# Two rates of a background stream of weight sums: 2.4 in place of 3.2 a tile before the first norm, 0.75 in place of 0.72 an item in the MLP

## The chip, the core and the metric

The kernel runs on one core of a Trainium2 chip. The metric is the time of one execution in microseconds (us), taken on the device; the time given for a kernel is the median of several runs. Before the change it is 1033.77 us (median of 3 runs, 1033.19 to 1034.73).

## What is computed

One layer of a decoder trunk on 512 tokens of width 1024, all in float32. The parts that matter here come after the three attention mixers:

```python
merged = (g[:, :, 0] * (o_da @ w_branch_da) + g[:, :, 1] * (o_sb @ w_branch_sb)
          + g[:, :, 2] * (o_dl @ w_branch_dil))
m = merged @ w_out
x = layer_norm(DEEPNORM_ALPHA * x + m, ln1_g, ln1_b)           # the first norm
hid = jax.nn.relu(x @ w_up)                                    # 1024 -> 4096
c = jnp.square(hid) @ w_down                                   # 4096 -> 1024
ple = jax.nn.sigmoid(x @ w_ple_gate) * (p @ w_ple)
x = layer_norm(DEEPNORM_ALPHA * x + c + ple, ln2_g, ln2_b)
```

## The kernel before, in words

**Products.** A float32 product is made of three TensorE (PE) products: each operand is cast to a rounded high part (ScalarE, ACT) and the rest is taken as its low part (VectorE, DVE); high times high, high times low and low times high are added up in PSUM. Large products are also split into quadrants and done with seven products of half size instead of eight (Strassen's scheme). For that the kernel needs sums and differences of weight quadrants, beside the weights themselves.

**Weight stream.** SyncE (SP) loads weights in chunks of 128x1024 (512 KB) into six buffers `raw`, in the order of use (line 213). For each chunk ACT makes `wh` (line 262) and DVE makes `wl` (line 264); of both there are five buffers. A buffer `raw` comes free when its `wl` is done, and the next load of SP waits for that.

**Sum steps.** The sums of weights are not made by the compute engines but by the DMA queue of GpSimd (POOL): `sum_steps()` (from line 1212) yields one DMA a step. A step copies 512 KB of a weight, or of an earlier sum, into a buffer in DRAM (line 1249), or adds 512 KB to it (line 1247). Buffers are `usum` for w_up, `dsum` for w_down, `gsum`, `qsum`, `msum`, `bsum` and `vsum` for others; eight steps make the four sums of one block of w_up or w_down, and 208 steps are issued in all. SP later loads such sums as chunks. A step that reads or adds to a buffer has to wait until the DMA before it on this buffer has landed. The wait is held by POOL, which takes its instructions strictly in their written order: whatever stands behind the step waits too. Besides, each step waits for the fourth last `wl` that was recorded before it, which spreads the steps over time.

**Order of the work.** The program is a list of items; an item is one PE product of a tile with what prepares it and what takes it out of PSUM. The main loop (from line 2177) walks through the items, and keeps a `credit`: before each item it adds `size * rate` (items 5 up to five behind the start of the output projection) or a constant (items from seven behind the start of the `w_ple` product to the end), and for each whole unit it issues one step. Between the two stretches, around the first norm, none is issued. The output projection starts at item 162, the `w_ple` product at item 174, the MLP's first item is near 200, and there are some 320 items. So the rate that the output projection's tiles carry counts only for its first five items, which are tile 0, two small transposes, tile 1 and one small transpose.

**The first norm.** For each of the four tiles of 128 tokens, `layer_norm_act` (from line 992) is: DVE makes the mean (`lnm`, line 997), ACT the squares (line 999), DVE the variance (`lr`, lines 1001 and 1002), POOL the power -1/2 of `lr` (line 1003, one 128x1 operation), DVE the result `xn` (line 1013, two instructions). `ln1_gen` then lets PE transpose the tile (line 1078, eight small products with `ident`), ACT cast it (`x1hT`, line 1084), DVE make its low part (`x1lT`, line 1085), and ACT copy it for the quadrants (`x1r`, line 1091). The gate product of the PLE branch (lines 1169 to 1171) comes next on PE; between the tiles' transposes stand the `w_ple` products (lines 1109 to 1111).

**POOL's other DMAs there.** `ln_g`, `ln_b` (line 988) and `pTr` (line 1780) are loads of constants; line 176 adds a quadrant of the gate's weights onto a `raw` buffer once its first form has been cast.

The two lines that the change touches, with what stands around them:

```python
item(cs if tt == 3 else [], mm, ev, need=cs, bank=at_bank)
items[-1]["rate"] = 3.2
...
if 5 <= n < wout_at + 5:
    credit += it["size"] * it.get("rate", 1.0)
elif n > ple_at + 6:
    credit += 0.72
while credit >= 1:
    credit -= 1
    next(sum_steps_, None)
```

Of the kernel before, what the change touches and what calls it, by code (L numbers as in the profile page):

```python
# [55 lines left out]
def trunk(tc, a, out):  # L56
    nc = tc.nc
    es = ExitStack()
    with es:
# [17 lines left out]
        def small(name, n):  # L77
            return one.tile([P, n], F32, name=nm(name), tag=f"sm{n}", bufs=12 if n < 8 else 8)
# [89 lines left out]
        def chunk(src, w):  # L168
            return chunk_of(load(src, w))
# [104 lines left out]
        def pump(limit, most=2):  # L274
            n = 0
            while n < most and st["split"] < len(chunks) and (chunks[st["split"]].get("aside")
                                                              or st["ring"] < limit + RING):
                fill()
                issue_split()
                n += 1  # L280
            fill()


        items = []

        def item(cs, mm, ev, need=None, bank=None, size=1.0):
            items.append({"c": cs, "mm": mm, "ev": ev, "need": need, "bank": bank, "size": size})
# [385 lines left out]
        def bring_back(i):  # L673
            for k in range(4 * i, 4 * i + 4):
                oT[k] = slot("oT")
                nc.sync.dma_start(oT[k], kept_oT.pop(k))
# [268 lines left out]
        def turn_item(h, th, kp):  # L945
            def mm(ps):
                for k in range(2):
                    for t in range(2):
                        o, c = k * 256 + t * P, (2 * kp + k) * P
                        nc.tensor.transpose(ps[:, o:o + P], merged[2 * th + t, h][:, c:c + P], ident)  # L950

            def ev(ps):
                hi, lo = slot("mh", F32R), slot("ml", F32R)
                nc.scalar.copy(hi, ps)
                nc.vector.tensor_sub(lo, ps, hi.bitcast(F32))
                merged_T[h, th, kp] = (hi, lo)
            item([], mm, ev, size=0.08)
# [70 lines left out]
        def wout_items():  # L1028
            for half in range(2):
                cs = [chunk(a["wo"][half, c].rearrange("p k n -> p (k n)"), 1024) for c in range(4)]  # L1030
                for tt in range(4):
                    ks = (4, 5, 6, 7, 0, 1, 2, 3) if tt == 2 and not half else range(8)

                    def mm(ps, tt=tt, cs=cs, ks=ks):
                        for k in ks:
                            c = cs[k // 2]
                            s = slice((k % 2) * 512, (k % 2) * 512 + 512)
                            h, lo = merged_T[k // 4, tt // 2, k % 4 // 2]
                            q = slice(k % 2 * 256 + tt % 2 * P, k % 2 * 256 + tt % 2 * P + P)
                            nc.tensor.matmul(ps, h[:, q], c["h"][:, s], start=k == ks[0], stop=False)  # L1040
                            nc.tensor.matmul(ps, h[:, q], c["l"][:, s], start=False, stop=False)
                            nc.tensor.matmul(ps, lo[:, q], c["h"][:, s], start=False, stop=k == ks[-1])

                    def ev(ps, tt=tt, half=half):
                        y = xn.pop((tt, half))
                        if not half:
                            x1sum[tt] = small("lsm", 2)
                        i = nc.vector.scalar_tensor_tensor(y, y, ALPHA, ps, op0=OP.mult, op1=OP.add,
                                                           accum_out=x1sum[tt][:, half:half + 1])
                        st["added"] = getattr(i, "ins", i)  # L1050
                        x1[tt, half] = y
                        if half:
                            pending.append(ln1_gen(tt))
                    item(cs if tt == 3 else [], mm, ev, need=cs, bank=at_bank)
                    items[-1]["rate"] = 3.2
                    for t in {0: [(1, 1, 0), (1, 1, 1)], 1: [(0, 1, 0), (0, 1, 1)]}.get(tt, ()) if not half else ():
                        turn_item(*t)

# [731 lines left out]
        def split_oT(i):  # L1790
            for k in range(4 * i, 4 * i + 4):
                oTs[k] = split(oT.pop(k), "oT")
# [348 lines left out]
        def step():  # L2141
            done = len(nc.cur_bb.bb.instructions)
            step_heads()
            for i in nc.cur_bb.bb.instructions[done:]:
                if i.engine in (mybir.EngineType.Activation, mybir.EngineType.DVE):
                    heads_last[i.engine] = i
            if tied[0]:
                tie[:] = list(heads_last.values())
# [24 lines left out]
        credit = 0.0  # L2173
# [3 lines left out]
        for n, it in enumerate(items):  # L2177
            if n == forms_at:
                pending.append(mixer_forms())
            if n == gated_at - 1:  # L2180
                while active or waiting:
                    step()
            for i in range(3):
                if i and n == branch_at[i] - (0, 9, 14)[i]:
                    bring_back(i)
                if n == branch_at[i] - (8, 2, 8)[i]:
                    while any(k not in ready for k in range(4 * i, 4 * i + 4)):
                        step()
                    if i == 1:
                        split_oT(i)  # L2190
                    else:
                        pending.append(branch_forms(i))
            need = it["need"] or it["c"]
            while any("h" not in c for c in need):
                before = st["split"]
                pump(freed, 1)
                assert st["split"] > before, n
            if prev is not None:
                prev[0]["ev"](prev[1])
                todo, lead = prev[0].get("then", ((), 0))  # L2200
                preps.extend(todo)
                for _ in range(lead):
                    left_step(*preps.popleft())

            pump(freed, {1: 3, 3: 0, 4: 0, ple_at: 0, ple_at + 1: 0}.get(n, 1 if n < 10 else 2))
            if n == 8:
                tie.clear()
            tied[0] = pair_at[1] + 12 <= n < gated_at
            if n == gated_at:
                tie.clear()  # L2210
            if n == 4:
                with tc.issue_after(st["load"]):
                    load_consts()
            if n == 10:
                with tc.issue_after(st["low"]):
                    make_lam()
            if n == 9:
                load_onehot()
            if n == 13:
                pending.append(tables())  # L2220

            if 5 <= n < wout_at + 5:
                credit += it["size"] * it.get("rate", 1.0)
            elif n > ple_at + 6:
                credit += 0.72
            while credit >= 1:
                credit -= 1
                next(sum_steps_, None)
            if n == 22:
                turn_tables()  # L2230
            if n == DA_TABS:
                da_tables()
            if n == DA_TABS + 6:
                turn_da()
            if n == wout_at + 1:
                load_pT()
            if n == ple_at - 3:
                with tc.issue_after(st["added"]), tc.issue_after(st["cast"]):
                    split_pT()
            if n == wout_at - 8:  # L2240
                load_xn(0)
            if n == wout_at - 4:
                load_xn(1)
            if n == wout_at - 1:
                ln_consts("ln1_g", "ln1_b")
            if n == ln2_at[0]:

                ln_consts("ln2_g", "ln2_b")
            for j in (n, n + 1):
                if j < len(items) and items[j].get("pre"):  # L2250
                    items[j].pop("pre")()
            if n > 1:
                step()
            ps = it["bank"]() if it["bank"] else mm_bank()
            for _ in it["mm"](ps) or ():
                if HALF:
                    step()
            freed += sum(not c.get("aside") for c in it["c"])

            pump(freed, 0 if n < 10 or ple_at - 1 <= n <= ple_at + 1 or n in sums_first else 2)  # L2260
            prev = (it, ps)
            if n + 1 < len(items) and n >= wout_at and pending:
                pass
# [113 lines left out]
```

## Time and profile before

| what | value |
|---|---|
| median of 3 runs | 1033.77 us (1033.19 to 1034.73) |
| the profiled execution's own time | 1031.9 us |
| its span, first to last instruction | 1030.2 us |
| granted TensorE clock, mean over the span | 0.997 |
| PE busy | 1016.4 us (99%) |
| DVE busy | 796.5 us (77%) |
| ACT busy | 614.7 us (60%) |
| POOL busy | 208.5 us (20%) |
| moved by DMA | 275.99 MB, 268 GB/s in the mean |
| POOL's DMA queue (q0) | 135.08 MB, 52.1% of 16 engines' span |
| SP's DMA queue (q1) | 138.99 MB, 36.8% |

The profiled execution is one of its own, 1.87 us below the median of the runs; 1.7 us of its time lie outside the span. Busy time of PE is modelled from the starts of pipelined products, so that products of 0.39 us each follow one another every 0.23 us. In a row of the timeline stand the start, the duration, engine, line, operation and tiles; "idle before" tells how long the engine had nothing to run, and what ended that. Buffer numbers are left out of tile names there.

### The profile page before, as it was taken

The page shows a single profiled execution, that of the slowest core. Times are in us where ns is not written, and L with a number is a line of the kernel's source. Part 1 is how long each engine was busy: PE and PEld are TensorE (multiplying, and loading weights), DVE is VectorE, ACT ScalarE, POOL GpSimd, SP SyncE. Part 2 cuts the span into 40 slices and gives each one's busy share as a digit, 9 for nine tenths or more (in the row PEclk, how much of TensorE's full clock was granted, in tenths as well). Part 3 has the DMA queues.
Part 4 walks back from the last instruction along what each step waited for, and adds up shares of the span by engine and source line. Part 5 has one row for each costly group of instructions (what it writes and reads, how often), then busy time and mean ns, then how long its engine had stood idle before and what let it go on. Part 6 is the DMA issues. An engine that isn't in the chain of part 4 may idle for free.

```text
span 1030.2 us, 15635 instructions
## 1 busy us (share of the span) xinstructions
PE 1016.4 (99%) x5626; PEld 880.8 (86%) x5626; DVE 796.5 (77%) x1411; ACT 614.7 (60%) x1055; POOL 208.5 (20%) x311
## 2 busy tenths in 40 slices
PE   9999999999999999999999999899999999999997
PEld 7888887788998898888888888789999899899886
DVE  6888697788657777787788876697768777777975
ACT  7566566775544656556655733776666556556651
POOL 0322320121412224111221140221121212111101
PEclk9999999999999999999999999999999999999999
DMA  8999993888899999989999994789999999999922
GB/s 311 282 308 287 254 269 103 208 209 266 275 322 276 274 279 273 286 222 299 284 270 299 305 306 162 171 236 333 322 322 345 301 347 306 328 313 292 310 79 82
DMA packets 79885, 275.99 MB, mean 268 GB/s; under 512 B 9816, under 2 KB 10600, under 8 KB 79808
## 3 DMA queue, kind: packets, MB, share of 16 engines
q0 software_dynamic: 37712, 135.08, 52.1%
q1 hardware_dynamic: 41520, 138.99, 36.8%
q8 instruction: 44, 0.72, 0.3%
q10 hardware_dynamic: 576, 0.92, 0.2%
q14 instruction: 33, 0.27, 0.1%
HBM read 267.59 MB, written 116.42 MB: 373 GB/s over the span
## 4 chain that ended last, share of the span: by engine, by line
PE 88%; DVE 3%; DMA 3%; issue 2%; ACT 2%; POOL 1%; DVEq 0%; POOLq 0%; ACTq 0%
PE mm L87 9%; PE mm L88 9%; PE mm L89 9%; PE at L1430 4%; PE at L1431 4%; PE at L1432 4%; PE at L750 2%; PE at L752 2%; PE at L751 2%; PE at L89 2%; PE at L88 2%; PE at L87 2%; PE mm L750 2%; PE mm L752 2%; PE mm L751 2%
## 5 line engine op out<-in xcount | busy, mean ns | idle before, releaser
L264 DVE TENSOR_TENSOR wl<-raw,wh 128x1024 fp32r<-128x1024 f32 (+1 forms) x274 | 330.3, 1214 | 105.0 <-ACT wh L262 103.7
L262 ACT CAST wh<-raw 128x1024 fp32r<-128x1024 f32 (+1 forms) x274 | 284.4, 1043 | 206.0 <-PE mm L88 104.3
L87 PE MATMUL mm<-xhT,wh 128*128 128x512 f32 (+1 forms) x254 | 95.5, 376 | 1.1 <-DVE dl_k L346 1.1
L89 PE MATMUL mm<-xhT,wl 128*128 128x512 f32 (+1 forms) x254 | 94.3, 371 | 0.0
L88 PE MATMUL mm<-xlT,wh 128*128 128x512 f32 (+1 forms) x254 | 94.1, 370 | 0.0
L1430 PE MATMUL at<-wh,hh 128*128 128x512 f32 x188 | 73.7, 392 | 0.0
L1431 PE MATMUL at<-wl,hh 128*128 128x512 f32 x188 | 73.7, 392 | 0.0
L1432 PE MATMUL at<-wh,hl 128*128 128x512 f32 x188 | 73.1, 389 | 0.0
L87 PE MATMUL mm<-x1hT,wh 128*128 128x256 f32 x256 | 72.8, 284 | 0.3 <-ACT up L1358 0.3
L89 PE MATMUL mm<-x1hT,wl 128*128 128x256 f32 x256 | 72.4, 283 | 0.0
L88 PE MATMUL mm<-x1lT,wh 128*128 128x256 f32 x256 | 72.4, 283 | 0.0
L87 PEld LDWEIGHTS mm<-xhT,wh 128*128 128x128 f32 x254 | 47.9, 189 | 8.9 <-issue 1.2
L89 PEld LDWEIGHTS mm<-xhT,wl 128*128 128x128 f32 x254 | 47.8, 188 | 8.2
L88 PEld LDWEIGHTS mm<-xlT,wh 128*128 128x128 f32 x254 | 47.9, 189 | 7.5
L1247 POOL DMA_DIRECT2D usum<-in_wu_dram x32 | 27.5, 861 | 120.8 <-DVE wl L264 43.9
L87 PEld LDWEIGHTS mm<-x1hT,wh 128*128 128x128 f32 x256 | 48.9, 191 | 2.3 <-ACT up L1358 0.5
L88 PEld LDWEIGHTS mm<-x1lT,wh 128*128 128x128 f32 x256 | 48.9, 191 | 1.5
L89 PEld LDWEIGHTS mm<-x1hT,wl 128*128 128x128 f32 x256 | 48.9, 191 | 0.0
L1247 POOL DMA_DIRECT2D dsum<-in_wd_dram x28 | 23.1, 824 | 120.4 <-DMA dsum<-dsum 32.4
L1432 PEld LDWEIGHTS at<-wh,hl 128*128 128x128 f32 x188 | 35.3, 188 | 7.6
L1430 PEld LDWEIGHTS at<-wh,hh 128*128 128x128 f32 x188 | 35.5, 189 | 6.2
L1431 PEld LDWEIGHTS at<-wl,hh 128*128 128x128 f32 x188 | 35.5, 189 | 5.7
(676 smaller groups left out, 2859.8 us busy)
## 6 DMA issues: line engine op xcount, KB each, us to landing
usum<-in_wu_dram POOLq DMA_DIRECT2D x48, 512.0 KB, 10.1
dsum<-in_wd_dram POOLq DMA_DIRECT2D x42, 512.0 KB, 9.1
raw<-usum SPq DMA_DIRECT2D x32, 512.0 KB, 9.1
raw<-dsum SPq DMA_DIRECT2D x28, 512.0 KB, 7.7
raw<-in_wt_dram SPq DMA_DIRECT2D x26, 512.0 KB, 7.2
raw<-in_wd_dram SPq DMA_DIRECT2D x25, 512.0 KB, 9.0
raw<-in_wu_dram SPq DMA_DIRECT2D x24, 512.0 KB, 8.8
qsum<-in_wq_dram POOLq DMA_DIRECT2D x18, 512.0 KB, 9.1
```

Source lines behind the costliest of these rows:

```text
L87: nc.tensor.matmul(ps, wh, xh, start=start, stop=False, skip_group_check=True)
L88: nc.tensor.matmul(ps, wh, xl, start=False, stop=False, skip_group_check=True)
L89: nc.tensor.matmul(ps, wl, xh, start=False, stop=stop, skip_group_check=True)
L262: i = nc.scalar.copy(h, raw)
L264: i = nc.vector.tensor_sub(lo, raw, h.bitcast(F32))
L750: nc.tensor.matmul(ps, h[:, q], c["h"][:, n], start=go, stop=False, skip_group_check=True)
L751: nc.tensor.matmul(ps, h[:, q], c["l"][:, n], start=False, stop=False, skip_group_check=True)
L752: nc.tensor.matmul(ps, lo[:, q], c["h"][:, n], start=False, stop=end, skip_group_check=True)
L1247: i = nc.gpsimd.dma_start(o, i, accum_op=OP.add, max_dma_last_dim=4096)
L1430: nc.tensor.matmul(ps, h[:, q], c["h"][:, s], start=go, stop=False, skip_group_check=True)
L1431: nc.tensor.matmul(ps, h[:, q], c["l"][:, s], start=False, stop=False, skip_group_check=True)
L1432: nc.tensor.matmul(ps, lo[:, q], c["h"][:, s], start=False, stop=end, skip_group_check=True)
```

## The change

The output projection's tiles carry a rate of 2.4 in place of 3.2, and the constant of the late stretch is 0.75 in place of 0.72. Nothing else is changed: the same 208 steps are issued in the same sequence, and the computation is the same.

```diff
                     item(cs if tt == 3 else [], mm, ev, need=cs, bank=at_bank)
-                    items[-1]["rate"] = 3.2
+                    items[-1]["rate"] = 2.4
...
             elif n > ple_at + 6:
-                credit += 0.72
+                credit += 0.75
```

The two tiles that count add 4.8 to the credit in place of 6.4. One step that was issued before item 165 is issued before item 181 (step 131, counted from 0: the copy `usum_3<-usum_1` of block 3 of w_up). The steps after it come one or two items later than before up to about item 205, level with before around items 213 to 239, and from item 241 on one, at the end two, items earlier (the last step before item 283 in place of 285). The orders of PE, DVE, ACT and SP stay the same; only POOL's changes, in two places and in one pair of neighbours near the end. With an item a step also gets another `wl` to wait for.

The first place is the first norm. POOL's rows from the constants' last load to the fourth tile's power, before the change (`lr` is the power of a tile, `raw` an addition onto a chunk, `usum` and `dsum` are sum steps; numbers at the end of names are buffers):

```order
L1780 DMA pTr_6403<-in_pT_dram 128x512
L1249 DMA usum_3_134<-usum_1_132 128x1024
L1003 TENSOR_TENSOR lr_6589<-lr_6589,mhalf 128x1
L1003 TENSOR_TENSOR lr_6629<-lr_6629,mhalf 128x1
L176 DMA raw_6367<-in_wg_dram 128x1024
L1003 TENSOR_TENSOR lr_6693<-lr_6693,mhalf 128x1
L1247 DMA dsum_1_156<-in_wd_dram 128x1024
L176 DMA raw_6527<-in_wg_dram 128x1024
L1247 DMA usum_3_134<-in_wu_dram 128x1024
L1249 DMA dsum_3_158<-dsum_1_156 128x1024
L1003 TENSOR_TENSOR lr_6739<-lr_6739,mhalf 128x1
```

and after it, on the same engine:

```order
L1780 DMA pTr_6402<-in_pT_dram 128x512
L1003 TENSOR_TENSOR lr_6588<-lr_6588,mhalf 128x1
L1003 TENSOR_TENSOR lr_6628<-lr_6628,mhalf 128x1
L176 DMA raw_6367<-in_wg_dram 128x1024
L1003 TENSOR_TENSOR lr_6692<-lr_6692,mhalf 128x1
L1249 DMA usum_3_134<-usum_1_132 128x1024
L176 DMA raw_6526<-in_wg_dram 128x1024
L1247 DMA dsum_1_156<-in_wd_dram 128x1024
L1003 TENSOR_TENSOR lr_6738<-lr_6738,mhalf 128x1
L1247 DMA usum_3_134<-in_wu_dram 128x1024
L1249 DMA dsum_3_158<-dsum_1_156 128x1024
```

The copy `usum_3<-usum_1` has moved behind the third power, and the addition to `usum_3` and the copy `dsum_3<-dsum_1`, which stood ahead of the fourth power, now stand behind it.

The second place is the end of the gate product, just ahead of the MLP. POOL's rows from the addition to `dsum_3` on, before the change:

```order
L1247 DMA dsum_3_158<-in_wd_dram 128x1024
L1249 DMA dsum_0_159<-in_wd_dram 128x1024
L176 DMA raw_6547<-in_wg_dram 128x1024
L176 DMA raw_6730<-in_wg_dram 128x1024
L1249 DMA dsum_2_161<-in_wd_dram 128x1024
L1249 DMA usum_0_135<-in_wu_dram 128x1024
```

and after it:

```order
L1247 DMA dsum_3_158<-in_wd_dram 128x1024
L176 DMA raw_6546<-in_wg_dram 128x1024
L176 DMA raw_6729<-in_wg_dram 128x1024
L1249 DMA dsum_0_159<-in_wd_dram 128x1024
L1249 DMA dsum_2_161<-in_wd_dram 128x1024
L1249 DMA usum_0_135<-in_wu_dram 128x1024
```

The copy into `dsum_0` has moved behind the two additions onto `raw`, so that three copies of sums now follow them, where there were two.

## The prediction

> **What bounds the kernel now.** The page comes first: it tells which engine is full.
>
> ```profile
> span 1030.2 us, 15635 instructions
> PE 1016.4 (99%) x5626; PEld 880.8 (86%) x5626; DVE 796.5 (77%) x1411; ACT 614.7 (60%) x1055; POOL 208.5 (20%) x311
> ```
>
> PE is busy for all but 13.8 us, so a change of POOL's order can gain only where PE stands still or runs slowly. The list of waits, for PE alone, says where:
>
> ```profile
> PE at L1169 <- ACT x1r L1091: 1.7, 1, 1.7
> ...
> PE at L1078 <- DVE xn L1013: 1.1, 1, 1.1
> ...
> PE mm L87 <- ACT up L1358: 0.3, 1, 0.3
> ```
>
> The first two rows belong to one place, the fourth tile of the first norm: the transposes (L1078) wait for `xn`, and the first gate product (L1169) for a copy of ACT. The table by stretches of time gives the granted clock there (the column before the last two; the last two are the DMA share and GB/s):
>
> ```profile
> 635.00:650.00 15.00, 15.00 (x76) 12.57 (x75) 11.53 (x23) 8.73 (x18) 0.98 (x2) 1.00 0.09 35
> 660.00:665.00 5.00, 2.19 (x12) 1.31 (x11) 3.15 (x4) 1.69 (x7) 0.73 (x2) 1.00 1.03 269
> 665.00:670.00 5.00, 5.00 (x16) 3.95 (x15) 3.00 (x4) 4.40 (x11) 0.85 (x1) 0.66 0.69 251
> ```
>
> After the standstill PE gets 0.66 of its clock for 5 us. Why `xn` is late is read from POOL's timeline:
>
> ```profile
> 620.36 0.54 POOL L1249 DMA_DIRECT2D usum<-usum  x1 [3.20 <-DMA usum<-in_wu_dram]
> ...
> 651.99 0.86 POOL L1247 DMA_DIRECT2D dsum<-in_wd_dram  x1
> ...
> 653.15 1.48 POOL L1247 DMA_DIRECT2D usum<-in_wu_dram  x1
> 659.59 0.56 POOL L1249 DMA_DIRECT2D dsum<-dsum  x1 [4.96 <-DMA dsum<-in_wd_dram]
> 660.16 0.58 POOL L1003 TENSOR_TENSOR lr<-lr,mhalf 128x1 f32<-128x1 f32 x1
> ```
>
> POOL stands 4.96 us with the copy `dsum<-dsum` until the addition issued at 651.99 has landed; the fourth tile's power stands behind it and starts at 660.16. DVE's timeline shows that its operand was there long before, and that DVE had nothing else to do:
>
> ```profile
> 640.25 0.14 DVE L1002 TENSOR_SCALAR lr<-lr 128x1 f32<-128x1 f32 x1
> 641.07 1.42 DVE L1013 SCALAR_TENSOR_TENSOR xn<-xn,lr,ln_b 128x512 f32<-128x512 f32 x2 [0.67 <-POOL lr L1003]
> ...
> 657.29 0.14 DVE L1002 TENSOR_SCALAR lr<-lr 128x1 f32<-128x1 f32 x1
> 660.78 1.41 DVE L1013 SCALAR_TENSOR_TENSOR xn<-xn,lr,ln_b 128x512 f32<-128x512 f32 x2 [3.34 <-POOL lr L1003]
> 662.11 1.22 DVE L264 TENSOR_TENSOR wl<-raw,wh 128x1024 fp32r<-128x1024 f32 x1
> 663.25 0.68 DVE L1085 TENSOR_TENSOR x1lT<-at,x1hT 128x512 fp32r<-128x512 f32 x1
> ```
>
> **The first norm, step by step.** After the change the addition to `usum_3` and the waiting copy `dsum<-dsum` stand behind the fourth power. What is left ahead of it are the copy `usum_3<-usum_1`, the two additions onto `raw` and the addition to `dsum`, all issued by about 654 as now. So the power starts when its operand is ready. The second tile gives the price of an open path: `lr` begins at 640.25 and `xn` at 641.07, 0.82 us later. For the fourth tile that makes 657.29 + 0.82 = 658.11 in place of 660.78: 2.67 us earlier.
>
> Does PE get all of it? ACT and PE around the place:
>
> ```profile
> 659.45 0.66 ACT L1084 CAST x1hT<-at 128x512 fp32r<-128x512 f32 x1
> 659.93 0.73 ACT L1091 COPY x1r<-at 128x256 f32<-128x256 f32 x2
> 663.96 0.65 ACT L1091 COPY x1r<-at 128x256 f32<-128x256 f32 x2 [3.31 <-DVE x1lT L1085]
> ```
>
> ```profile
> 649.10 1.03 PE L1078 MATMUL at<-ident,xn 128*128 128x128 f32 x8
> 649.89 0.48 PE L1109 MATMUL mm<-wh,pTh 128*128 128x512 f32 x1
> ...
> 659.98 0.39 PE L1110 MATMUL at<-wl,pTh 128*128 128x512 f32 x1
> 660.21 0.39 PE L1111 MATMUL at<-wh,pTl 128*128 128x512 f32 x1
> 661.68 1.29 PE L1078 MATMUL at<-ident,xn 128*128 128x128 f32 x8 [1.08 <-DVE xn L1013]
> 664.66 0.50 PE L1169 MATMUL at<-wh,x1hT 128*128 128x512 f32 x1 [1.70 <-ACT x1r L1091]
> ```
>
> L1169 waits for the PSUM bank that ACT's last copy `x1r` of the third tile frees at 664.61. That copy waits for `x1lT`, which stands in DVE's queue behind the fourth tile's `xn` and a `wl`. All of this moves with `xn`: `wl` to 659.44, `x1lT` to 660.58 (its operand `x1hT` is done at 660.11), the copy to 661.29, L1169 to 661.99. The transposes need a bank too, which the copies of 659.93 free at 660.66 at the latest, and take 0.79 us (649.10 to 649.89), so they are done by 661.45. Without any wait L1169 would come at 660.21 + 0.23 + 0.79 = 661.23; what stays is 0.76 us of standing still. **The start of the gate product gains 664.66 − 661.99 = 2.67 us.**
>
> The clock is the second part: 0.66 for 5 us loses 0.34 × 5 = 1.7 us of work. I expect no low stretch when two pauses of 0.2 us (660.44 to 660.66) and 0.5 us (661.45 to 661.99) take the place of 1.08 and 1.70.
> By the Trainium skill, *TensorE: Matmul & The Clock Gate*, section "Part 1: The HAM clock gate", the clock is halved after at least one idle window of some 3.4 us; no pause here is that long, so by that rule taken literally the dip has another cause, and only 2.67 us would be gained; what that makes of the time is the first rival below. The trace speaks against the literal reading: the clock fell right behind pauses of 1.08 and 1.70 us.
>
> **Sum at this place: 2.67 + 1.7 = 4.37 us.** Behind it, the next operands on the gate's path are the split forms `t7`:
>
> ```profile
> 677.30 0.39 PE L1169 MATMUL at<-wh,t7h 128*128 128x512 f32 x1
> 672.92 0.69 DVE L292 TENSOR_TENSOR t7l<-x1r,t7h 128x512 fp32r<-128x512 f32 x1
> ```
>
> They are ready at 673.61 for 677.30, 3.69 us early. DVE's chain moves by 2.67 and PE by 4.37, so 2.0 us are left.
>
> **The moved step itself.** Its price comes from the page's table of DMA queues (packets, MB, share of 16 engines):
>
> ```profile
> q0 software_dynamic: 37712, 135.08, 52.1%
> q1 hardware_dynamic: 41520, 138.99, 36.8%
> ```
>
> 512 KB leave the time of 620 and come at 652. POOL's queue q0 spends 52.1% of 1030.2 us on 135.08 MB, that is 4.0 us per MB or 2.1 us a step; SP's q1 36.8% on 138.99 MB, 1.4 us a load. The DMA engines have room right before (share 0.09 from 635 to 650), but POOL issues nothing there. PE's list above names no wait for a load at the norm or in the gate product, so the loads that were asked for earlier hide the step and I cost it at nothing; without that cover it would be 2.1 us.
>
> **The entry of the MLP.** From 684 on the DMA engines are full, and one load is just late:
>
> ```profile
> 666.00:684.00 18.00, 18.00 (x75) 14.80 (x74) 16.54 (x23) 15.10 (x26) 4.23 (x6) 0.92 0.71 177
> 690.00:730.00 40.00, 39.70 (x272) 36.89 (x271) 30.81 (x40) 25.21 (x38) 6.81 (x10) 1.00 1.04 337
> ```
>
> ```profile
> 707.90 1.05 ACT L262 CAST wh<-raw 128x1024 fp32r<-128x1024 f32 x1 [1.35 <-DMA raw<-usum]
> ```
>
> This is the 0.3 us of PE's list. With PE 4.37 us earlier, loads and steps are asked for earlier too, since both wait for `wl`. The DMA work up to there is the same and has to fit into less time: from 666 to 684 there is room of 0.29 × 18 = 5.2 us, and 4.37 are taken from it. That is close. Steps come one or two items later than now, which helps the loads a little; three copies in a row in place of two hurt. Bounds: −0.3 (the wait goes) to +2.1 (one more step ahead of a load). I charge 0.3 us, nearer to the row of today.
>
> **0.75 in place of 0.72.** It makes up for the step that was left out, and ends two items earlier. In the late MLP SP waits for sums:
>
> ```profile
> SPq L213 <- DMA dsum<-in_wd_dram: 9.7, 2, 7.9
> ```
>
> 7.9 us for one load, yet PE's list has no wait there: the loads ahead cover it. So a shorter wait of SP gains nothing, and somewhat denser steps cost nothing as long as casts wait for PE rather than for loads. Grouped for all casts from 690 to 985, what ended ACT's idle time is:
>
> ```profile
> PE mm L88: 63.5, 29
> PE at L88: 14.4, 8
> PE at L1432: 14.2, 14
> ...
> DMA raw<-usum: 1.3, 1
> ```
>
> One cast waited for a load, 51 in these rows for PE. I take 0, between −0.3 and +1.4 (one load).
>
> **Sum.** −4.37 + 0.3 = −4.1 us on the span of 1030.2, so 1026.1, and on the profiled time 1031.9, so 1027.8. That execution lies 1.87 below the median of the runs, to which I add the same difference: **1033.77 − 4.1 = 1029.7 us.**
>
> **Rivals.**
> *The clock dip stays.* Its window does not follow from PE's pauses alone, or 0.76 us are still enough. Then −2.67 + 0.3 = −2.4, 1031.4 us. Against it: the dip begins right behind the two pauses. Chance 0.12.
> *The DMA engines take it back.* If loads at the entry of the MLP land when they land now, because the queues are full from 684 on, PE waits there for what it gained: between −2 and 0, say 1032.9. For: the share of 1.04 from 690 to 730. Against: 51 idle times ended by PE in the rows above against one by a load, and the room of 5.2 us. Chance 0.15.
> *Slower: the loads queue behind POOL's copies.* The chain `usum_3`, `dsum_3` now starts behind the fourth power, and `dsum_0` joins the burst just as the first w_up loads are issued: two more steps ahead of them, 2 × 2.1 = 4.2 us for the load at 707.90, which has no reserve. A pause of over 3 us brings the clock dip back, 1.7 us: 5.9 lost against 4.37 gained, +1.5 us, 1035.3; one step more makes 1037.4. It decides once the loads land so late that PE's pause and the dip together cost over 4.4 us. Against: the steps are later, not more, and share the time with the loads in two queues. Chance 0.08.
> By the Trainium skill, *DMA: Bandwidth & Descriptors*, section "Queues, rings and completion order", a DMA engine takes packets from its queues in turn; by that a load stands behind about one step at a time, 2.1 us and not 4.2. No row here shows the alternation.
> *The change does nothing:* the fourth power is still held, by the addition onto `raw` or the addition to `dsum` issued before it. Then 1033.8. Against: both were issued in under 1.5 us by 654. Chance 0.05.
>
> **How the numbers follow.** The forecast has the remaining 0.60. Its own range: best −4.37 − 0.3 − 0.76 = −5.4, worst −4.37 + 2.1 = −2.3; with 0.6 us for the spread of the runs, 1027.8 to 1032.1. Taking in the clock rival and the better half of the DMA rival, 1027.8 to 1032.6 holds some 0.8. About 0.2%, 2.1 us, is what a measurement of this kernel can tell from no change: faster means below 1031.7. The forecast gives 0.57 to that (0.03 to same), the clock rival 0.09 (0.03 to same), the DMA rival 0.05 (0.10 to same), no effect 0.05 to same, the slower rival 0.07 (0.01 to same): 0.71 faster, 0.22 same, 0.07 slower.
>
> **What would show it.** In the profile after: the fourth `lr` of L1003 starting within 0.2 us of DVE's L1002; PE's wait at L1169 below 1 us and at L1078 below 0.4; a granted clock of 1.00 from 660 to 675; L1169's first product near 662.0; the cast at the MLP's entry still ended by a load for at most 2 us. It is wrong if that cast, or several behind it, wait 3 us or more for loads, if the clock dips all the same, or if the fourth power still starts near 660.

## The result, and the profile after

The changed kernel takes **1028.1 us** (median of 6 runs, 1027.6 to 1029.2); the kernel before 1032.85 us (the three runs given above and three taken beside the kernel after, 1031.1 to 1034.7). The ratio is 0.9957, with a 95% interval from 0.9945 to 0.9968, which is 4.4 us (3.3 to 5.7). One execution, among the 12 of the last experiment below, took 1252.7 us at a mean clock of 0.753; it is left out of every figure here. The profiled execution took 1027.65 us with a span of 1025.9, where before it was 1031.9 with 1030.2. PE's sum is what moved on the page, by 1.8 us, and the remaining 2.5 us of the 4.3 are time in which PE stood still:

```profile
span 1025.9 us, 15640 instructions
PE 1014.6 (99%) x5626; PEld 879.5 (86%) x5626; DVE 796.0 (78%) x1411; ACT 614.1 (60%) x1055; POOL 208.2 (20%) x311
```

PE's list of waits (in total, times, longest) has lost the row of L1078, and that of L1169 has gone from 1.7 to 0.5; the wait for `up` at the entry of the MLP, 0.3 before, is 0.2:

```profile
PE at L1169 <- ACT x1r L1091: 0.5, 1, 0.5
...
PE mm L87 <- ACT up L1379: 0.2, 1, 0.2
```

POOL's timeline shows why. The fourth power stands at 657.63 and the addition and the copy behind it:

```profile
652.10 0.59 POOL L1249 DMA_DIRECT2D usum<-usum  x1
652.68 0.91 POOL L176 DMA_DIRECT2D raw<-in_wg_dram  x1
653.27 1.20 POOL L1247 DMA_DIRECT2D dsum<-in_wd_dram  x1
657.63 0.56 POOL L1003 TENSOR_TENSOR lr<-lr,mhalf 128x1 f32<-128x1 f32 x1 [3.17 <-DVE lr L1002]
661.07 0.84 POOL L1247 DMA_DIRECT2D usum<-in_wu_dram  x1 [2.88 <-DVE wl L264]
665.97 0.55 POOL L1249 DMA_DIRECT2D dsum<-dsum  x1 [4.06 <-DMA dsum<-in_wd_dram]
```

The bracket tells who is waited for. Before the fourth power POOL now waits for DVE, whose result it needs; the wait of 4 to 5 us for `dsum` to land is still there, at 665.97, but no power stands behind it. DVE's operation that makes the operand starts at 657.40, 0.23 us ahead of the power (2.87 before):

```profile
657.40 0.15 DVE L1002 TENSOR_SCALAR lr<-lr 128x1 f32<-128x1 f32 x1
658.23 1.42 DVE L1013 SCALAR_TENSOR_TENSOR xn<-xn,lr,ln_b 128x512 f32<-128x512 f32 x2 [0.68 <-POOL lr L1003]
```

PE's timeline and the table by stretches (the third figure from the right is the granted clock) close the chain. The gate product starts at 662.11, and the stretch that had 0.66 of the clock has all of it:

```profile
660.53 1.03 PE L1078 MATMUL at<-ident,xn 128*128 128x128 f32 x8
662.11 0.50 PE L1169 MATMUL at<-wh,x1hT 128*128 128x512 f32 x1 [0.54 <-ACT x1r L1091]
```

```profile
660.00:665.00 5.00, 4.46 (x25) 3.56 (x24) 2.36 (x3) 4.34 (x11) 0.84 (x1) 1.00 1.05 293
665.00:670.00 5.00, 5.00 (x24) 4.14 (x23) 4.56 (x8) 4.64 (x10) 0.55 (x1) 1.00 0.98 292
```

The start of the first power differs by a microsecond or two from execution to execution, so two stretches say more than a clock time: from the first power (L1003) to the first gate product (L1169), and from there to the end of the span. Before and after, POOL's first power:

```profile
634.87 0.57 POOL L1003 TENSOR_TENSOR lr<-lr,mhalf 128x1 f32<-128x1 f32 x1 [13.97 <-DVE lr L1002]
```

```profile
634.98 0.57 POOL L1003 TENSOR_TENSOR lr<-lr,mhalf 128x1 f32<-128x1 f32 x1 [18.13 <-DVE lr L1002]
```

The first stretch was 664.66 − 634.87 = 29.79 us and is 662.11 − 634.98 = 27.13; the second was 1030.2 − 664.66 = 365.5 and is 1025.9 − 662.11 = 363.8. The change gave 2.66 us in the norm and 1.7 behind it, less 0.1 that this execution came later to the norm.

### The profile page after: what moved, and what is told of

Read it like the earlier page. It is cut to its first block, busy times and chain, and to the rows that moved or that the text cites. A ratio compares the mean times of both kernels' runs of the same rounds, so it can differ in the third digit from the quotient of the medians.

```text
span 1025.9 us, 15640 instructions
## 1 busy us (share of the span) xinstructions
PE 1014.6 (99%) x5626; PEld 879.5 (86%) x5626; DVE 796.0 (78%) x1411; ACT 614.1 (60%) x1055; POOL 208.2 (20%) x311
## 4 chain that ended last, share of the span: by engine, by line
PE 85%; DVE 6%; issue 3%; DMA 3%; ACT 2%; POOL 1%; DVEq 0%; POOLq 0%; ACTq 0%
PE mm L87 8%; PE mm L88 8%; PE mm L89 8%; PE at L1430 4%; PE at L1431 4%; PE at L1432 4%; DVE wl L264 2%; PE at L750 2%; PE at L751 2%; PE at L752 2%; PE mm L750 2%; PE mm L752 2%; PE mm L751 2%; PE at L89 2%; PE at L88 2%
```

## The experiments

The theory: the gain is POOL's hold at the fourth power, and the dip of the clock that PE's pauses bring; nothing else in the change matters. The rivals are the other things that the change does (the rate of the MLP, a step less at 620 us, later sums), and that the dip has another cause. All kernels differ from the one before, except where it says otherwise. Their numbers together ("held" is from the start of DVE's last L1002 to the start of the fourth power; the stretches are those of the one profiled execution, the medians and ratios those of all):

| kernel | held | power to gate product | gate product to end | median, us | ratio to before (95%) |
|---|---|---|---|---|---|
| before | 2.87 | 29.79 | 365.5 | 1032.0 to 1032.9 | |
| after | 0.23 | 27.13 | 363.8 | 1028.1 | 0.9957 (0.9945–0.9968) |
| 2.4 alone | 0.23 | 27.14 | 363.6 | 1027.9 | 0.9955 (0.9942–0.9967) |
| 0.75 alone | 2.71 | 29.63 | 366.3 | 1031.9 | 0.9992 (0.9983–1.0001) |
| swap alone | 0.23 | 27.13 | 363.6 | 1028.1 | 0.9957 (0.9944–0.9971) |
| rate 4.0 | 1.61 | 28.27 | 364.1 | 1029.2 | 0.9967 (0.9954–0.9979) |
| rate 3.6 | 0.23 | 26.59 | 365.1 | 1028.8 | 0.9968 (0.9958–0.9979) |
| first pause filled | 3.04 | 29.97 | 365.1 | 1031.0 | 0.9988 (0.9979–0.9997) |
| second pause filled | 2.71 | 29.63 | 363.8 | 1030.9 | 0.9988 (0.9979–0.9997) |
| after, 1.2 from item 200 | 0.23 | 27.15 | 364.4 | 1029.5 | 0.9977 (0.9966–0.9988) |
| rate 4.8 | 0.23 | see there | 363.5 | 1032.2 | 0.9996 (0.9988–1.0005) |
| rate 0.8 | 0.24 | 26.60 | 365.1 | 1027.1 | 0.9954 (0.9940–0.9968) |
| rate 4.8, late start | 0.24 | see there | 363.6 | 1032.6 | 1.0001 (0.9991–1.0012) |

### The two numbers apart

```diff
-                    items[-1]["rate"] = 3.2
+                    items[-1]["rate"] = 2.4
```

> 2.4 in the first norm alone, the MLP at 0.72 as before. Theory (POOL's hold at the fourth lr power is all of it): the fourth L1003 starts within 0.2 us of DVE's L1002, PE's waits at L1078 and L1169 shrink from 1.08 + 1.70 to about 0.5 us, no half clock from 660 to 675, so -4.3 us against before, give or take 0.5; the sums stay one item late to the end of the MLP, which may cost up to 0.5. Rival 1 (the 0.75 carries it, because sums that come late hold loads back): no gain here, 0 or a loss. Rival 2 (the load on the DMA engines is what counts): between the two, about -2.

```diff
-                credit += 0.72
+                credit += 0.75
```

> 0.75 in the MLP alone, 3.2 in the first norm as before. Theory: the fourth lr power is held as before (start near 660.2), the dip of the clock stays, and denser steps cost and bring nothing: 0 us, between -0.5 and +0.5. Rival 1 (0.75 carries the gain): -4. Rival 3 (denser steps take DMA time from the loads of the MLP): +1 to +2.

2.4 alone gives all of the gain, 0.75 alone nothing that can be told from no change. In the kernel with 0.75 alone POOL's rows read as before, with the copy's wait ahead of the power:

```profile
659.09 0.56 POOL L1249 DMA_DIRECT2D dsum<-dsum  x1 [4.79 <-DMA dsum<-in_wd_dram]
659.66 0.58 POOL L1003 TENSOR_TENSOR lr<-lr,mhalf 128x1 f32<-128x1 f32 x1
```

### The swap alone

```diff
-            elif n > ple_at + 6:
+            elif n > ple_at + 7:
```

> Rates 3.2 and 0.72 as before; the count of the MLP starts one item later, so that the fourth lr power stands just ahead of the copy dsum_3<-dsum_1 on POOL; no step leaves the place at 620 us. Theory (who stands behind the waiting copy decides): the whole gain, -4.3 us, give or take 0.5, with the fourth L1003 within 0.2 us of L1002. Rival 2 (moving a step's 512 KB away from 620 us relieves the DMA engines): no gain, 0. Rival 4 (the start of the MLP's steps is what matters, not the norm): a gain without a change of the fourth L1003.

Here the rates are those of before; the steps of the MLP start one item later, which is enough to put the fourth power ahead of the copy, while the copy `usum_3` stays in the norm. POOL's rows, with that copy first:

```profile
620.17 0.54 POOL L1249 DMA_DIRECT2D usum<-usum  x1 [3.47 <-DMA usum<-in_wu_dram]
...
658.46 0.56 POOL L1003 TENSOR_TENSOR lr<-lr,mhalf 128x1 f32<-128x1 f32 x1 [2.96 <-DVE lr L1002]
663.57 0.59 POOL L1249 DMA_DIRECT2D dsum<-dsum  x1 [4.54 <-issue]
```

The whole gain, with both stretches as in the kernel after. So the 512 KB that leave the time of 620 are worth nothing that these runs can tell, and what stands ahead of the power carries the gain.

### More steps ahead: 4.0 and 3.6

```diff
-                    items[-1]["rate"] = 3.2
+                    items[-1]["rate"] = 4.0
```

> 4.0 in place of 3.2 in the first norm, 0.72 in the MLP: more steps ahead, so that another waiting step, the addition of w_down onto dsum_3, stands ahead of the fourth lr power; it waits for the landing of the copy dsum_3<-dsum_1. Theory: POOL is held again, 2 to 6 us by how late that copy is issued; the fourth L1003 starts 1 us or more behind L1002, and the time is that of before or longer, 0 to +2 us. Rival 5 (it is the particular copy, or the number of steps between the norm's items, and fewer or more would both do): as after, -4.

```diff
-                    items[-1]["rate"] = 3.2
+                    items[-1]["rate"] = 3.6
```

> 3.6 in place of 3.2 in the first norm, 0.72 in the MLP. The copy dsum_3<-dsum_1 stands ahead of the fourth lr power as before, but the addition to dsum_1 for which it waits is issued ahead of the whole norm, near 620 us, and has landed long before. Theory (the wait holds POOL, not the copy): the fourth L1003 starts within 0.2 us of DVE's L1002, L1169 starts 27.1 us behind the first L1003 (29.7 before), no half clock, so -4.3 us, give or take 0.5. Rival (a DMA copy ahead of the power costs by itself, or an earlier step at 620 us costs what it does): no gain.

The expectation for 4.0 was wrong: it is faster than before by some 3.4 us. The hold came back, but smaller. POOL's rows, and DVE's operand:

```profile
649.61 0.84 POOL L1249 DMA_DIRECT2D dsum<-dsum  x1
...
656.93 0.84 POOL L1247 DMA_DIRECT2D dsum<-in_wd_dram  x1 [5.03 <-DMA dsum<-dsum]
657.49 0.87 POOL L1003 TENSOR_TENSOR lr<-lr,mhalf 128x1 f32<-128x1 f32 x1
```

```profile
655.88 0.14 DVE L1002 TENSOR_SCALAR lr<-lr 128x1 f32<-128x1 f32 x1
```

The copy for which this addition waits was issued at 649.61, ahead of a `raw`, 15.6 us behind the first power (at 634.00 here), while in the kernel before the awaited addition went out at 651.99, 17.1 us behind it. The wait of POOL is as long as before, 5.03 us, but it begins earlier, and only its last 0.9 us fall behind the end of DVE's operation (656.02 to 656.93); with the issue of the addition itself the power starts 1.6 us behind the start of that operation. That this earlier start would shrink the hold could have been read from the order; the expectation counted the step and not its time. And PE stands still once, without a dip: it waits nowhere at L1078, waits 1.67 us at L1169, and has its whole clock.

```profile
662.27 0.50 PE L1169 MATMUL at<-wh,x1hT 128*128 128x512 f32 x1 [1.67 <-ACT x1r L1091]
```

```profile
665.00:670.00 5.00, 5.00 (x24) 4.14 (x23) 4.56 (x8) 4.63 (x10) 0.00 (x0) 1.00 0.70 252
```

With 3.6 the same copy as before stands ahead of the fourth power, but the addition that it waits for was issued 30 us ahead of it. POOL issues it at once and the power is on time:

```profile
622.45 0.85 POOL L1247 DMA_DIRECT2D dsum<-in_wd_dram  x1 [0.74 <-issue]
...
653.13 0.88 POOL L1249 DMA_DIRECT2D dsum<-dsum  x1
657.64 0.56 POOL L1003 TENSOR_TENSOR lr<-lr,mhalf 128x1 f32<-128x1 f32 x1 [3.63 <-DVE lr L1002]
```

So it is the wait, not the copy. The last 0.5 us of waiting at L1169 is gone too (26.59): here, as with 0.8 below, the third power starts 0.24 or 0.25 us behind the start of its L1002, in the kernel after 1.08 us; that the one follows from the other was not tested. But the second stretch is 1.3 us longer than that of the kernel after, and by the runs this kernel gains 3.3 us, less than the expectation's 4.3, give or take 0.5. Two pauses of PE at the entry of the MLP, 1.05 us together where the kernel after has one of 0.15, make most of it; each stands behind a cast that waits for a load. PE's rows, then ACT's:

```profile
703.82 0.39 PE L87 MATMUL mm<-x1hT,wh 128*128 128x256 f32 x1 [0.41 <-ACT up L1358]
706.15 0.39 PE L87 MATMUL mm<-x1hT,wh 128*128 128x256 f32 x1 [0.64 <-ACT up L1358]
```

```profile
701.96 1.05 ACT L262 CAST wh<-raw 128x1024 fp32r<-128x1024 f32 x1 [1.65 <-DMA raw<-usum]
704.78 1.05 ACT L262 CAST wh<-raw 128x1024 fp32r<-128x1024 f32 x1 [1.02 <-DMA raw<-usum]
```

This is what the prediction's rival of the DMA engines describes, at the place that it named and at less than half of its price. Why these two loads come late was not isolated; with 4.8, below, still more steps are issued early, and PE has no such pause.

### The dip by itself

These two leave the hold as it is and only give PE something to do in a pause: idle transposes of the identity, whose results are overwritten or never read.

```diff
                 tp = at_bank()
+                if tt == 3 and not h:
+                    for b in range(8):
+                        nc.tensor.transpose(tp[:, b % 4 * P:b % 4 * P + P], ident, ident)
                 for b in range(4):
```

> The kernel before with eight idle transposes of the identity ahead of the fourth tile's transposes (L1078), into the same bank, which the real ones then overwrite: they fill PE's first pause of 1.08 us. POOL's hold stays, so L1169 still starts 29.7 us behind the first L1003 and still waits about 1.7 us. Theory (the dip of the clock comes from the two pauses together; the rate of 4.0 had the second alone and no dip): no half clock, and the time from L1169 to the end shrinks from 365.5 to about 364 us, so -1.5 us, between -2.2 and -1.0. Rival 1 (the dip comes from the long pause alone, or from something else than PE's work): the dip stays, 0. Rival 2 (transposes do not count as work): the dip stays, 0.

```diff
+            if tt == 3:
+                idle = mm_bank()
+                for b in range(12):
+                    nc.tensor.transpose(idle[:, b % 4 * P:b % 4 * P + P], ident, ident)
             for h in range(2):
                 for kp in range(2):
```

> The kernel before with twelve idle transposes of the identity into a spare bank behind the fourth tile's transposes: they fill most of PE's second pause (1.70 us, at L1169), and leave the first (1.08 us). POOL's hold stays, L1169 still starts 29.7 us behind the first L1003. Theory: no half clock, -1.5 us, between -2.2 and -1.0. Rival 1 (the pauses have no part in the dip) and rival 2 (transposes do not count as work): the dip stays, 0.

In the second kernel L1169 starts where it did, 29.63 us behind the first power, and the clock stays whole, so that the second stretch is that of the kernel after, 363.8:

```profile
661.57 1.29 PE L1078 MATMUL at<-ident,xn 128*128 128x128 f32 x8 [0.92 <-DVE xn L1013]
662.70 1.47 PE L1089 MATMUL mm<-ident 128*128 128x128 f32 x12
664.55 0.50 PE L1173 MATMUL at<-wh,x1hT 128*128 128x512 f32 x1 [0.38 <-ACT x1r L1095]
```

```profile
665.00:670.00 5.00, 5.00 (x24) 4.12 (x23) 3.10 (x5) 4.63 (x10) 0.85 (x1) 1.00 0.72 267
```

Only PE's pause was filled and the gate product starts where it did, so the pauses are what brings the dip. In the first kernel the profiled execution still had it, behind pauses of 0.28 and 1.69 us:

```profile
662.40 1.38 PE L1081 MATMUL at<-ident,xn 128*128 128x128 f32 x8 [0.28 <-DVE xn L1013]
665.48 0.78 PE L1172 MATMUL at<-wh,x1hT 128*128 128x512 f32 x1 [1.69 <-ACT x1r L1094]
```

```profile
665.00:670.00 5.00, 4.52 (x13) 3.65 (x14) 2.18 (x3) 4.52 (x11) 0.85 (x1) 0.66 0.70 244
```

The expectation of no half clock failed there. All executions tell more. Each one lists its clock averaged over the span, and a dip of 3.41 us to half takes 0.0017 from it. The clock is at half behind PE's last products too, for 1.8 to 4.9 us of the span in the 13 profiles, which takes 0.0009 to 0.0024; so 0.997 or less tells of a dip besides, if narrowly. The five profiled executions with a dip in the norm list 0.996 or 0.997, the eight without one 0.998 or 0.999. Of the 63 executions of the kernel before that stand beside these experiments, 47 have 0.997 or less; with 0.75 alone 7 of 11; of the kernel after 0 of 6, with the swap alone 0 of 5, with 4.0 0 of 5, with the second pause filled 0 of 11, and with the first filled 3 of 11. So the dip is a matter of chance, with odds that the pauses set; 3 of 11 is too few to be told from the zeros, but all of these lie far below 47 of 63. In the kernel before, executions with 0.997 or less have a median of 1032.65 us, the others 1031.17: 1.5 us for a dip, 1.1 us on the mean of all. The list is rough: one of the 47 has 0.946 at an ordinary time of 1033.2 us. Both filled kernels gained about that, 1.2 us (0.3 to 2.2).

The length of a dip varies too. In the profile of 0.75 alone the clock is at half from 663.2 to 670.0, 6.8 us and so twice 3.41, and its second stretch is the longest of all, 366.3:

```profile
660.00:665.00 5.00, 2.38 (x12) 1.59 (x11) 3.15 (x4) 1.86 (x7) 0.24 (x1) 0.82 1.04 288
665.00:670.00 5.00, 5.00 (x13) 3.83 (x13) 3.51 (x5) 3.52 (x9) 0.85 (x1) 0.50 0.67 250
```

### Denser steps in the MLP

```diff
-                credit += 0.75
+                credit += 0.75 if n < 200 else 1.20
```

> The kernel after with 1.2 in place of 0.75 an item from item 200 on: steps of the MLP much denser, the norm as after. Theory of the prediction (denser steps cost nothing as long as casts wait for PE): the time of after, -4.3 us against before, give or take 0.6. Rival (steps that come early take DMA time from the loads): PE waits in the MLP for loads, one or two of 1 to 2 us each, so -3 to -1 against before.

The edit is on the kernel after. It is 1.4 us slower than that by the medians, with intervals that just overlap, and its 2.4 us against before lie in the range of the rival (3 to 1), not in that of the theory. Its second stretch is 0.6 us longer than that of the kernel after, and a pause of 0.74 us, where that kernel has 0.15, accounts for it; PE waits behind a cast that waited for its load at the entry of the MLP:

```profile
714.04 1.05 ACT L262 CAST wh<-raw 128x1024 fp32r<-128x1024 f32 x1 [1.01 <-DMA raw<-in_wu_dram]
```

```profile
715.41 0.39 PE L87 MATMUL mm<-x1hT,wh 128*128 128x256 f32 x1 [0.74 <-ACT up L1379]
```

Denser steps are not free without limit: 0.03 more cost nothing that was measured, 0.45 more cost this pause.

### Far more and far fewer

```diff
-                    items[-1]["rate"] = 3.2
+                    items[-1]["rate"] = 4.8
```

> 4.8 in place of 3.2 in the first norm, 0.72 in the MLP: the whole chain of copies and additions up to dsum_3 is issued ahead of the norm, and what stands among the powers are copies that wait for no landing. Theory (a wait on POOL ahead of the fourth power costs, the number of steps does not): the fourth L1003 within 0.2 us of L1002, L1169 27.1 us or less behind the first L1003, no half clock: -4.3 us, give or take 0.6. The rate of 3.6 lost 1.05 us at the entry of the MLP, where two casts waited for loads; by the theory that goes if fewer steps are left there, by the rival (more steps early crowd the loads) it grows to 2 us, so -2.5.

```diff
-                    items[-1]["rate"] = 3.2
+                    items[-1]["rate"] = 0.8
```

> 0.8 in place of 3.2 in the first norm, 0.72 in the MLP: nothing that waits for a landing stands ahead of the fourth power, and the sums run two to three steps late to the end. Theory: norm as after, -4.3 us against before, less what late sums cost in the MLP: SP waits for dsum tiles up to a few us, of which the loads ahead cover most, so -4.3 to -3. Rival (the change works by having the steps later, the more the better): -5 or better.

```diff
-                    items[-1]["rate"] = 3.2
+                    items[-1]["rate"] = 4.8
...
-            elif n > ple_at + 6:
-                credit += 0.72
+            elif n > ple_at + 12:
+                credit += 0.75
```

> 4.8 in the first norm and a start of the MLP's steps six items later, at 0.75: no step at all stands among the norm's powers, and the entry of the MLP has fewer of them. Theory: the fourth power free, and no cast waiting for a load at the entry: L1169 26.6 us behind the first L1003 and 363.6 us from there to the end, -4.5 us against before, so the time of after or up to 0.8 less. Rival (steps at 620 us or late sums cost as much): the time of after plus 1.

The two kernels with 4.8 were expected to be 4.3 and 4.5 us faster and are not faster at all, although the fourth power is on time in both. The hold has gone to the **first** power. POOL and DVE with 4.8:

```profile
629.52 0.54 POOL L1249 DMA_DIRECT2D dsum<-dsum  x1 [2.61 <-DMA dsum<-in_wd_dram]
639.08 0.81 POOL L1247 DMA_DIRECT2D dsum<-in_wd_dram  x1 [9.02 <-DMA dsum<-dsum]
639.64 0.86 POOL L1003 TENSOR_TENSOR lr<-lr,mhalf 128x1 f32<-128x1 f32 x1
```

```profile
635.07 0.15 DVE L1002 TENSOR_SCALAR lr<-lr 128x1 f32<-128x1 f32 x1
640.53 1.42 DVE L1013 SCALAR_TENSOR_TENSOR xn<-xn,lr,ln_b 128x512 f32<-128x512 f32 x2 [5.31 <-POOL lr L1003]
```

The addition to `dsum_3` waits 9.02 us for its copy to land, and the first power starts 4.57 us behind its operand. PE waits twice 1.4 and once 0.5 us in the norm, and the dip is back, at 0.66 in the stretch from 660:

```profile
PE at L1078 <- ACT ple L1115: 1.4, 1, 1.4
PE at L1078 <- DVE xn L1013: 1.4, 1, 1.4
...
PE at L1109 <- ACT x1r L1091: 0.5, 1, 0.5
```

```profile
660.00:665.00 5.00, 4.50 (x15) 3.47 (x14) 4.32 (x7) 5.00 (x14) 0.56 (x1) 0.66 1.01 324
```

From DVE's first L1002 to the gate product it takes 667.00 − 635.07 = 31.93 us, which with the dip inside is 1.9 more than before (30.03); behind it 363.5 us, 2.0 less than before with its dip there. The sum is nothing, and so is what was measured. With the later start the hold is at the same place and longer, 5.29 us (the first power at 639.62, its L1002 at 634.33). 8 of 11 executions have a mean clock of 0.997 or less in each of the two. The expectation had looked at the fourth power only; the theory behind it, that a waiting DMA ahead of a power costs, stands, and is stronger for having been found at another one.

With 0.8 nothing waits ahead of any power, and the norm is as with 3.6 (26.60, no wait at L1169). The sums are two to three steps late to the end: SP's waits for `dsum` grow from 13.9 us in the kernel after to 19.5, and PE has one pause of 1.0 us in the profiled execution, whose time, 1029.73 us, is the longest of the six. SP's row, then PE's:

```profile
SPq L213 <- DMA dsum<-in_wd_dram: 19.5, 2, 10.1
```

```profile
PE at L1431 <- DVE wl L264: 1.0, 1, 1.0
```

By its runs it cannot be told from the kernel after (0.9954 against 0.9957); its gain of 4.7 us lies 0.4 above the expected range and below the 5 of the rival, and its interval holds both. No version tried beats the kernel after by more than a measurement can tell; 2.4 alone, the swap alone, 0.8 and the change as it was made are one result.

## Why the prediction was right, point by point

- **The hold.** The step of the prediction: the fourth power 0.2 us behind L1002, L1169 at 661.99 with 0.76 us of standing still, 2.67 us gained. Measured: 0.23 us, 662.11 with 0.54, and 2.66 us between first power and gate product. The 0.2 us less of standing still are the short pause that was expected ahead of the transposes; they started without one. The swap alone shows that this is the cause, 3.6 that it is the wait and not the copy, and 4.8 that the first power can be hit as well.
- **The clock.** 1.7 us were put down for a dip that goes with the pauses. In the two profiled executions it is 1.7 (365.5 against 363.8). Over all executions it is 1.1, since only three in four had a dip to lose: the prediction took as certain what is a matter of chance. On the mean its term is 0.6 us too large, and the term of the MLP's entry, below, is 0.45 off the other way; that the sum comes out so well is in part luck. The rival by which the dip stays is refuted by the second pause filled: same start of the gate product, no dip, some 1.2 us less. By the Trainium skill, *TensorE: Matmul & The Clock Gate*, section "Part 1: The HAM clock gate", the activity window is free-running, and the point at which the clock changes depends on where in the window the first matmul lands. The counts agree with such a window: the same kernel has the dip in 47 of 63 executions. The idle window of some 3.4 us that the page asks for is not needed in one piece here: 1.08 and 1.70 us, with transposes between them, were enough.
- **The moved step at nothing.** Right: the swap alone leaves it where it was and gives the same time, within the interval.
- **0.75 at nothing.** Right, both ways: 0.75 alone 0.9992 (0.9983 to 1.0001), and 2.4 without it as fast as with it. The words behind it, that somewhat denser steps cost nothing, hold for 0.75 and not for 1.2.
- **The entry of the MLP.** 0.3 us were charged for a longer pause; PE's pause there went from 0.30 to 0.15. This is the one term of the sum that had the wrong sign. It is 0.45 us off, more than the whole difference between the forecast of 4.1 and the 4.3 of the spans. The cast that the prediction watched waits for PE now, and the one whose load is late is a later one, by 0.43 us, so neither the rival of the DMA engines nor the slower one came. The mechanism is real: with 3.6 the pauses there were 1.05 us and with 1.2 from item 200 on 0.74. ACT's row of the later cast, in the kernel after:

```profile
712.36 1.05 ACT L262 CAST wh<-raw 128x1024 fp32r<-128x1024 f32 x1 [0.43 <-DMA raw<-in_wu_dram]
```

- **The level.** The profiled execution was forecast at 1027.8 us and took 1027.65. The median was forecast at 1029.7, 1.6 above the 1028.1 that were measured. The term that was too large is the 1.87 us by which the first three runs of the kernel before lay above its profiled execution. The 66 times of the kernel before that were taken beside the kernel after and the experiments have a median of 1032.2 us, 0.3 above that execution.

## What to carry to other kernels

Where an engine issues DMAs and computes, look in its timeline for a DMA that waits for another DMA's landing, and at what stands behind it: here a power of 0.6 us, on an engine that is busy 20% of the time, set the pace of an engine at 99%. Do not judge such a schedule by how many steps lie ahead, but by whether the awaited transfer has landed when the engine comes to the wait; with 3.6 the awaited addition had been out for 30 us and there was no hold, with 4.0 an issue 1.5 us earlier took 1.3 us off it, and with 4.8 it moved to another power. A short pause of PE can cost more than its length, and whether it does is a matter of chance: count executions, don't trust one profile.

## What the runs showed of the hardware

- The clock dip needs no long pause. Pauses of 1.08 + 1.70 us within 4.1 us brought it in 47 of 63 executions, 0.28 + 1.69 with 16 transposes around in 3 of 11, 0.92 + 0.38 in 0 of 11, a single one of 1.67 in 0 of 5 (the pauses are those of the profiled execution). Where between these the bound lies was not measured.
- In the norm the clock was at half for 3.4 us in four of the five profiles with a dip, and for 6.8 us in the fifth (0.75 alone).
- Transposes of 128x128 can keep the clock up: with twelve of them in 1.47 us in the second pause the dip went from 47 of 63 executions to 0 of 11.
- The time from the issue of a copy of 512 KB to its landing, as the next step saw it, was 7.3 us when issued at 649.61 and 9.6 us at 629.52 (from the issue of the copy to that of the addition, with 4.0 and with 4.8), and 7.7 us with 4.8 and the later start. A step counted on to be done in 7 us can hold its engine for two more.
